# Where the two parts of each weight tile lie against the activations, modulo 256 bytes

## The chip, the cores and the metric

The kernel runs on one core of a Trainium2 chip. The metric is the device time of one execution in microseconds; the time before is the median of three runs.

## The reference, cut to what matters

The reference is a decoder trunk of two layers over 256 tokens of width 2048, in float32. Layer 0 mixes tokens by gated linear attention (GLA), layer 1 by forgetting attention (FoX); each mixer is followed by a gated MLP with a short convolution. Nearly all the arithmetic is in products of the 256 tokens with large weight matrices:

```python
for i in range(DEPTH):                                   # 2 layers
    mod = (cond @ w_mod[i] + b_mod[i])                   # shifts, scales and gates, 6 x 2048, from one vector
    h = rmsnorm(x, norm_mix[i]) * (1.0 + sc_m) + sh_m
    y = gla_mixer(h, ...)  or  fox_mixer(h, ...)         # h @ w_in (2048 x 6160, or 2048 x 8208), attention, @ w_out
    x = x + (1.0 + g_m) * y
    h = rmsnorm(x, norm_ffn[i]) * (1.0 + sc_f) + sh_f
    x = x + (1.0 + g_f) * conv_ffn(h, ...)               # h @ w_up (2048 x 11264), conv, silu(gate) * val, @ w_down (5632 x 2048)
return rmsnorm(x, norm_final)
```

## The kernel before

**The products.** Weights stream from HBM once, in tiles of 128 rows by 1024 columns (512 KB), through a ring of five tiles named `w` that they share with the tiles `wm` of the modulation matrix. `plan` is a list of these tiles in the order of their use, and `next_w` loads them ahead by that list. Each tile is split by `split_w` into two parts of the type float32r: ScalarE casts it to `wh` (L110), VectorE subtracts to get the rest, `wl` (L111). Activations are split in the same manner into a high and a low part (the tiles `h`, made by `make_h`, and `op`, made by `raw_operand`). A product is then three matmuls: high by high, high weight by low activation, low weight by high activation.

**Which operand is held.** A matmul has one operand that is loaded into the array (128 columns, by an instruction LDWEIGHTS of its own, which the profile calls PEld) and one that moves through it. In `stream_a` the weights are held, in blocks of 128 columns, and the 256 tokens move: three matmuls of 256 columns for each block of weights and row tile (L540, L541, L542). It serves nearly everything: the GLA projections but v, both output projections, both MLPs, and the output gate of FoX. In `stream_b` the activations are held and the weights move, 512 columns at a time (L573 to L575): v of GLA and q, k, v of FoX. `narrow` (L587 to L589) serves the projections of 16 columns; it holds weights like `stream_a`.

```python
nc.tensor.matmul(o, wh[:, ms], rh, ...)      # L540, stream_a: out, held, moving; ms = 128 columns, 512 bytes
nc.tensor.matmul(o, wh[:, ms], rl, ...)      # L541
nc.tensor.matmul(o, wl[:, ms], rh, ...)      # L542

cs = slice((k - kts[0]) * nn, (k - kts[0]) * nn + P)   # narrow: nn = 16 columns, a step of 64 bytes for each k
nc.tensor.matmul(pa[:, :T], nh[:, cs], lh, ...)        # L587; L588 has nh and ll, L589 nl and lh
```

**Positions.** Every tile has a fixed byte position in each of the 128 partitions of the on-chip memory. In the program before, the tiles `w`, `h`, `op`, `wh` and `wl` all start at 160 modulo 256 bytes, and the blocks that `stream_a` and `stream_b` take from them step by 512 or 1024 bytes, so a held block and a moving block are always at the same position modulo 256. `narrow` alone is different: its held block lies 64 bytes further for each row tile k, so its offset against the activations runs through 0, 64, 128, 192 and round again. The tiles follow a DMA scratch of 16,384 bytes and fill nearly all that the program may use.

**The order around it.** The program is written out straight, and the order on each engine is set when it is built. `tick` puts a paced share of other work behind each row tile: sums of the modulation vectors on VectorE (L248), convolutions, attention. The buffers hold four tiles each of `wh` and `wl` (AHEAD + 1), so the split runs up to three row tiles ahead of the matmuls; a cast (L110) waits until the matmuls have finished with the buffer that it writes.

Of the kernel before, what the change touches and what calls it, by code (L numbers as in the profile page):

```python
# [59 lines left out]
ORDERED = ("v",)  # L60
NBIG = 12


@with_exitstack
def kernel(
# [37 lines left out]
    def t1(s="t1"):  # L103
        return tmp.tile([P, T], F32, tag="t1", bufs=T1, name=nm(s))

    def split_w(src):
        n_ = src.shape[-1]
        hi = tmp.tile([P, 1024], F32R, tag="wh", bufs=AHEAD + 1, name=nm("wh"))[:, :n_]
        lo = tmp.tile([P, 1024], F32R, tag="wl", bufs=AHEAD + 1, name=nm("wl"))[:, :n_]
        nc.scalar.copy(out=hi, in_=src)  # L110
        order["v"] = nc.vector.tensor_tensor(out=lo, in0=src, in1=hi.bitcast(F32), op=ALU.subtract).ins  # L111
        return hi, lo
# [1 line left out]
    def misc():  # L114
        return psM.tile([P, 512], F32, tag="m" if PS[1] else "a", name=nm("pm"))

# [1 line left out]
    ident = const.tile([P, P], F32, name="ident")  # L118
    make_identity(nc, ident)
    identr = const.tile([FH, FH], F32R, name="identr")  # L120
# [8 lines left out]
    nc.vector.tensor_scalar_mul(mgla, tri, 1.0 / 16.0)  # L129
    nc.vector.memset(mgla[0:CH, CH:P], 0.0)  # L130

# [1 line left out]
    crow = ringt([P, P], "crow")  # L133
    nc.sync.dma_start(out=crow[:KT, :], in_=c.rearrange("b (r p) -> (b r) p", p=P))
    rows = ringt([P, P], "rows")
# [59 lines left out]

    bfc = const.tile([FH, 1], F32, name="bfc")

# [1 line left out]
    mod = const.tile([P, 12, KT], F32, name="mod")  # L199
    bg = deque()  # L200

# [9 lines left out]
        return es  # L211

    def mod_tasks(l, key, f0=0, fn=D, wide=False, direct=0, defer=False):
        # columns of silu(c) @ w_mod + b_mod, finished as the layer uses them;
        # the first `direct` row tiles are summed on the tensor engine, the others on the vector engine
        s = SECT[key]
        width = fn // -(-fn // 1024)
        per = 1
# [120 lines left out]
        pace["bg"] = (len(bg) + len(pending)) / float(n_halves)  # L339
        pace["acc"] = 0.0  # L340

# [1 line left out]
    def rsqrt(dst, src, scale, nn):  # L343
        v = tmp.tile([P, 16], F32, tag="rs_v", name=nm("rv"))
        t = tmp.tile([P, 16], F32, tag="rs_t", name=nm("rt"))
# [19 lines left out]
            nc.tensor.matmul(pb[:, i * P:(i + 1) * P], ones, dg, start=True, stop=True)  # L365
        return pb

# [1 line left out]
    xT = const.tile([P, KT, T], F32, name="xT")  # L369

    def load_x():
# [37 lines left out]
                                              skip_group_check=True).ins  # L409

    def token_rstd():
        # columns of -1/sqrt(mean + eps), one per token tile
        v = tmp.tile([P, 2], F32, tag="tv", name=nm("tv"))
        t = tmp.tile([P, 2], F32, tag="tt", name=nm("tt"))
        q = tmp.tile([P, 2], F32, tag="tq", name=nm("tq"))
        nc.vector.tensor_scalar(out=v, in0=ss["p"][:, :2], scalar1=0.5 / D, scalar2=0.5 * EPS,
                                op0=ALU.mult, op1=ALU.add)
        nc.vector.tensor_scalar(out=q.bitcast(I32), in0=v.bitcast(I32), scalar1=1, scalar2=None,
                                op0=ALU.logical_shift_right)
        nc.vector.tensor_scalar(out=q.bitcast(I32), in0=q.bitcast(I32), scalar1=-1.0,  # L420
                                scalar2=float(0x5F3759DF - 0x00400000), op0=ALU.mult, op1=ALU.add)
        for _ in range(3):
            for i in range(2):
                c1 = slice(i, i + 1)
                nc.vector.tensor_scalar(out=t[:, c1], in0=q[:, c1], scalar1=q[:, c1], scalar2=v[:, c1],
                                        op0=ALU.mult, op1=ALU.mult)
            for i in range(2):
                c1 = slice(i, i + 1)
                nc.vector.tensor_scalar(out=q[:, c1], in0=t[:, c1], scalar1=1.5, scalar2=q[:, c1],
                                        op0=ALU.subtract, op1=ALU.mult)  # L430
        return q
# [48 lines left out]
            return st["t"][:, 0, k % 4, :], st["t"][:, 1, k % 4, :]  # L480
        return lazy(make, nk, 2)

# [1 line left out]
    plan = []  # L484

    def plan_stream(w, kts, cols):
        for kt in kts:
            plan.append((w, kt, 1, tuple(cols)))

    gate = {"n": 0, "ins": []}  # L490
    fetched = {"load": 0, "split": 0, "use": 0}
# [2 lines left out]
    def next_w(kt, cols, hold=None):  # L494
        i = fetched["use"]
        assert plan[i][1] == kt and plan[i][3] == tuple(cols), (plan[i][1:], kt, cols)
        fetched["use"] += 1
        run, look = AHEAD if hold is None else hold, RING - 1
        if i < STAGE:
            run, look = min(run, STAGE - i), 1  # L500
        while fetched["split"] < min(i + 1 + run, len(plan)):
            while fetched["load"] < min(fetched["split"] + look, len(plan)):
                w_, kt_, nk_, cols_ = plan[fetched["load"]]
                fetched["load"] += 1
                wt = ringt([P, 1024])
                o = 0
                for c0, cn in cols_:
                    if nk_ == 1:
                        with after_startup():
                            nc.sync.dma_start(out=wt[:, o:o + cn], in_=w_[kt_ * P:(kt_ + 1) * P, c0:c0 + cn])  # L510
                        o += cn
                    else:
                        nc.sync.dma_start(out=wt[:, :nk_ * cn].rearrange("p (k r) -> p k r", r=cn),
                                          in_=w_[kt_ * P:(kt_ + nk_) * P, c0:c0 + cn]
                                          .rearrange("(k p) r -> p k r", p=P))
                        nc.vector.memset(wt[:, nk_ * cn:nk_ * cn + P - cn], 0.0)
                        o = nk_ * cn + P - cn
                raws.append(wt[:, :o])
            with ExitStack() as es:
                if gate["n"] > 0:  # L520
                    gate["n"] -= 1
                    for ins in gate["ins"]:
                        es.enter_context(tc.issue_after(ins))
                splits.append(split_w(raws.popleft()))
            fetched["split"] += 1
        return splits.popleft()

# [1 line left out]
        return [psA.tile([P, 2, T], F32, tag="a", name=nm("pa")) for _ in range(4)]  # L529

    def stream_a(kts, cols, rhs, done=None):
        # with done: the last TAIL rows are multiplied output by output, so that done(pair) can follow early
        ps = banks()
        held = []

        def mms(m, k, wh, wl, rh, rl):
            first, last = k == kts[0], k == kts[-1]
            ms = slice(m * P, (m + 1) * P)
            o = ps[m // 2][:, m % 2, :]
            nc.tensor.matmul(o, wh[:, ms], rh, start=(first and m % 2 == 0), stop=False, skip_group_check=True)  # L540
            nc.tensor.matmul(o, wh[:, ms], rl, start=False, stop=False, skip_group_check=True)  # L541
            nc.tensor.matmul(o, wl[:, ms], rh, start=False, stop=last, skip_group_check=True)  # L542

        for k in kts:
            rh, rl = rhs(k)
            tail = done is not None and k in kts[-TAIL:]
            wh, wl = next_w(k, cols, kts[-1] - k + 1 if tail else None)
            if tail:
                held.append((k, wh, wl, rh, rl))
                continue  # L550
            for m in range(8):
                mms(m, k, wh, wl, rh, rl)
            tick()
        if done is not None:
            for m in range(8):
                for args in held:
                    mms(m, *args)
                if m % 2 == 1:
                    done(m // 2, ps)
        return ps  # L560
# [50 lines left out]
    ALL = list(range(KT))  # L611

    def log_sigmoid(dst, z, e, bias=None):
        # z may be in PSUM; min(z, 0) - log(1 + exp(-|z|))
        nc.scalar.activation(e, z, AF.Abs)
        nc.scalar.activation(e, e, AF.Exp, scale=-1.0)
        nc.scalar.activation(e, e, AF.Ln, bias=1.0)
        nc.vector.scalar_tensor_tensor(out=dst, in0=z, scalar=0.0, in1=e, op0=ALU.min, op1=ALU.subtract)

# [1 line left out]
    def gla(l, h):  # L621
        parts = {}
        pieces = [("a", 6144), ("q", 0), ("k", 1024), ("v0", 2048), ("v1", 3072), ("r0", 4096), ("r1", 5120)]
# [233 lines left out]
        set_pace(N1)  # L857
        add_residual(l, "g_m", ALL, rhs)

# [1 line left out]
    def fox(l, h):  # L861
        pf = narrow(ALL, 4 * D, FH, h)
        lf = t1("lf")[:FH, :]
# [166 lines left out]
        pace["side"], pace["sacc"] = 1.0, 0.0  # L1030
        add_residual(l, "g_m", ALL, rhs)

# [1 line left out]
    def ffn(l, h, first_blocks):  # L1034
        act = [bigt([P, 8, T], "act") for _ in range((FT + 7) // 8)]

# [76 lines left out]
            cs = slice(m * P, (m + n_) * P)  # L1113
            nc.vector.tensor_tensor(out=fin["o"][tt][:, cs], in0=pt[:, :n_ * P], in1=fin["g"][:, cs], op=ALU.mult)

# [1 line left out]
    def plan_ffn(l):  # L1117
        w = ffn_w_up[l]
        groups = []
# [17 lines left out]
    for nb in BLOCKS:  # L1137
        for i, c0 in enumerate((0, 1024, 2048, 3072, 4096, 5120)):
            if i == (0 if k0 + nb == KT else 1):
                plan.append((gla_w_in[0], k0, nb, ((6144, RANK),)))  # L1140
            plan_stream(gla_w_in[0], range(k0, k0 + nb), [(c0, 1024)])
        k0 += nb
    for g in range(2):
        plan_stream(gla_w_out[0], ALL, [(g * 1024, 1024)])
    plan_ffn(0)
    plan.append((fox_w_in[0], 0, KT, ((4 * D, FH),)))
    for c0 in (2 * D, 2 * D + 1024, 0, D, 1024, D + 1024, 3 * D, 3 * D + 1024):
        plan_stream(fox_w_in[0], ALL, [(c0, 1024)])
    for g in range(2):
        plan_stream(fox_w_out[0], ALL, [(g * 1024, 1024)])  # L1150
    plan_ffn(1)
# [107 lines left out]
```

## Time and profile before

| what | before |
|---|---|
| time, median of 3 runs (range) | 2566.05 us (2564.85 to 2567.67) |
| span of the profiled execution, first to last instruction | 2570.5 us |
| matmuls busy, of the span | 2515.7 us, 98% (19242 matmuls) |
| VectorE busy | 1912.2 us, 74% |
| ScalarE busy | 1280.2 us, 50% |
| HBM traffic | 638 MB, 248 GB/s on average |
| matmuls with held weights in `stream_a` | 3 x (3584 + 1920) = 16512, of 256 columns |
| matmuls with moving weights in `stream_b` | 3 x 512 = 1536, of 512 columns |

The profiled execution has no other time than its span; it is 4.5 us above the median of the timed runs, and above the slowest of them by 2.8 us. Matmuls overlap in the records (each lasts longer than the distance to the next), so what one of them costs is read as the distance between starts in the timeline, not as its duration.

### The profile page before, as it was taken

The page shows a single profiled execution, that of the slowest core. Times are in us where ns is not written, and L with a number is a line of the kernel's source. Part 1 is how long each engine was busy: PE and PEld are TensorE (multiplying, and loading weights), DVE is VectorE, ACT ScalarE, POOL GpSimd, SP SyncE. Part 2 cuts the span into 40 slices and gives each one's busy share as a digit, 9 for nine tenths or more (in the row PEclk, how much of TensorE's full clock was granted, in tenths as well). Part 3 has the DMA queues.
Part 4 walks back from the last instruction along what each step waited for, and adds up shares of the span by engine and source line. Part 5 has one row for each costly group of instructions (what it writes and reads, how often), then busy time and mean ns, then how long its engine had stood idle before and what let it go on. Part 6 is the DMA issues. An engine that isn't in the chain of part 4 may idle for free.

```text
span 2570.5 us, 47584 instructions
## 1 busy us (share of the span) xinstructions
PE 2515.7 (98%) x19242; PEld 2431.0 (95%) x19242; DVE 1912.2 (74%) x2570; ACT 1280.2 (50%) x1956; POOL 14.6 (1%) x35
## 2 busy tenths in 40 slices
PE   6999999999999999999999999999999999999998
PEld 6988899899999999999988889999999999999998
DVE  7767988876679998877587888777766667666544
ACT  2446454445555656543454555444545555565332
POOL 0000000000000000000000000000000000000000
PEclk7999999999999999999999999999999999999999
DMA  8897978798668888889489887686777767756553
GB/s 337 282 301 226 304 245 285 261 321 299 182 183 272 296 295 286 277 310 309 153 285 311 299 265 238 227 278 202 220 223 215 222 212 229 221 183 204 181 181 115
DMA packets 184313, 638.36 MB, mean 248 GB/s; under 512 B 23961, under 2 KB 24971, under 8 KB 183708
## 3 DMA queue, kind: packets, MB, share of 16 engines
q1 hardware_dynamic: 183704, 635.17, 74.9%
q8 instruction: 150, 2.46, 0.4%
q14 instruction: 71, 0.58, 0.1%
q10 hardware_dynamic: 388, 0.15, 0.0%
HBM read 633.14 MB, written 2.10 MB: 247 GB/s over the span
## 4 chain that ended last, share of the span: by engine, by line
PE 85%; DMA 7%; DVE 4%; issue 2%; ACT 1%; DVEq 0%; SPq 0%; ACTq 0%
PE pa L542 23%; PE pa L541 23%; PE pa L540 23%; DMA wm<-in_w_mod_dram 5%; PE pa L574 4%; PE pa L573 4%; PE pa L575 4%; DVE wl L111 2%; DVE acc L248 1%; DMA w<-in_ffn_w_down_dram 1%; DMA w<-in_gla_w_out_dram 1%; ACT wh L110 1%; PE pm L261 1%; DMA w<-in_gla_w_in_dram 0%; PE pm L777 0%
## 5 line engine op out<-in xcount | busy, mean ns | idle before, releaser
L110 ACT CAST wh<-w 128x1024 fp32r<-128x1024 f32 x819 | 855.1, 1047 | 1138.2 <-PE pa L541 677.6
L111 DVE TENSOR_TENSOR wl<-w,wh 128x1024 fp32r<-128x1024 f32 x819 | 995.6, 1219 | 455.7 <-ACT wh L110 444.6
L540 PE MATMUL pa<-h,wh 128*128 128x256 f32 x3584 | 1012.6, 285 | 5.6 <-ACT h L461 5.6
L542 PE MATMUL pa<-h,wl 128*128 128x256 f32 x3584 | 1015.0, 285 | 2.6 <-DVE wl L111 2.6
L541 PE MATMUL pa<-h,wh 128*128 128x256 f32 x3584 | 1015.8, 284 | 1.0 <-DVE h L463 0.9
L540 PEld LDWEIGHTS pa<-h,wh 128*128 128x128 f32 x3584 | 688.0, 193 | 6.8 <-ACT h L461 6.5
L542 PEld LDWEIGHTS pa<-h,wl 128*128 128x128 f32 x3584 | 688.8, 193 | 5.8 <-DVE wl L111 3.3
L541 PEld LDWEIGHTS pa<-h,wh 128*128 128x128 f32 x3584 | 690.1, 193 | 1.7 <-DVE h L463 1.4
L541 PE MATMUL pa<-op,wh 128*128 128x256 f32 x1920 | 540.4, 284 | 1.9 <-DVE op L479 1.9
L540 PE MATMUL pa<-op,wh 128*128 128x256 f32 x1920 | 539.6, 284 | 1.9 <-ACT wh L110 1.6
L248 DVE SCALAR_TENSOR_TENSOR acc<-wm,cT,acc 128x1024 f32<-128x1024 f32 x352 | 450.8, 1281 | 110.0 <-DMA wm<-in_w_mod_dram 109.4
L542 PE MATMUL pa<-op,wl 128*128 128x256 f32 x1920 | 530.2, 284 | 0.1
L541 PEld LDWEIGHTS pa<-op,wh 128*128 128x128 f32 x1920 | 369.3, 192 | 2.1 <-DVE op L479 2.1
L540 PEld LDWEIGHTS pa<-op,wh 128*128 128x128 f32 x1920 | 368.5, 192 | 2.5 <-ACT wh L110 2.0
L542 PEld LDWEIGHTS pa<-op,wl 128*128 128x128 f32 x1920 | 363.1, 192 | 0.7 <-DVE wl L111 0.7
L574 PE MATMUL pa<-wh,h 128*128 128x512 f32 x512 | 201.1, 393 | 0.0
L573 PE MATMUL pa<-wh,h 128*128 128x512 f32 x512 | 199.5, 393 | 0.9 <-ACT wh L110 0.9
L575 PE MATMUL pa<-wl,h 128*128 128x512 f32 x512 | 193.1, 394 | 0.0
L573 PEld LDWEIGHTS pa<-wh,h 128*128 128x128 f32 x512 | 96.6, 189 | 20.8 <-ACT wh L110 1.3
L574 PEld LDWEIGHTS pa<-wh,h 128*128 128x128 f32 x512 | 96.5, 189 | 19.8 <-issue 0.2
L575 PEld LDWEIGHTS pa<-wl,h 128*128 128x128 f32 x512 | 96.2, 189 | 19.1
L1039 ACT ACTIVATE y<-u,cw 128x256 f32<-128x256 f32 x176 | 101.6, 599 | 4.8 <-DVE act L1055 2.4
(236 smaller groups left out, 1389.9 us busy)
## 6 DMA issues: line engine op xcount, KB each, us to landing
wm<-in_w_mod_dram SPq DMA_DIRECT2D x352, 512.0 KB, 5.0
w<-in_ffn_w_up_dram SPq DMA_DIRECT2D x320, 512.0 KB, 4.3
w<-in_ffn_w_down_dram SPq DMA_DIRECT2D x176, 512.0 KB, 4.5
w<-in_fox_w_in_dram SPq DMA_DIRECT2D x128, 512.0 KB, 5.0
w<-in_gla_w_in_dram SPq DMA_DIRECT2D x96, 512.0 KB, 5.1
wm<-in_w_mod_dram SPq DMA_DIRECT2D x16, 1024.0 KB, 12.3
w<-in_gla_w_out_dram SPq DMA_DIRECT2D x32, 512.0 KB, 5.6
w<-in_ffn_w_up_dram SPq DMA_DIRECT2D x64, 256.0 KB, 3.9
```

Of the source, the lines that this page charges most:

```text
L110: nc.scalar.copy(out=hi, in_=src)
L111: order["v"] = nc.vector.tensor_tensor(out=lo, in0=src, in1=hi.bitcast(F32), op=ALU.subtract).ins
L248: nc.vector.scalar_tensor_tensor(out=st["a"], in0=wt[:, j, :], scalar=col, in1=st["a"], op0=ALU.mult, op1=ALU.add)
L261: nc.tensor.transpose(pt[:, m * P:(m + 1) * P], st["a"][:, (q0 + m) * P:(q0 + m + 1) * P], ident)
L540: nc.tensor.matmul(o, wh[:, ms], rh, start=(first and m % 2 == 0), stop=False, skip_group_check=True)
L541: nc.tensor.matmul(o, wh[:, ms], rl, start=False, stop=False, skip_group_check=True)
L542: nc.tensor.matmul(o, wl[:, ms], rh, start=False, stop=last, skip_group_check=True)
L573: nc.tensor.matmul(o, lh[:, ts_], wh[:, hs_], start=first, stop=False)
L574: nc.tensor.matmul(o, ll[:, ts_], wh[:, hs_], start=False, stop=False)
L575: nc.tensor.matmul(o, lh[:, ts_], wl[:, hs_], start=False, stop=last)
L1039: nc.scalar.activation(y, u, AF.Identity, scale=cw[:, l * 3 + 2, r:r + 1], bias=cw[:, 6 + l, r:r + 1])
```

## The change

Each of `wh` and `wl` gets a tile of 1088 columns instead of 1024. Where the weights are held (`moving` is false), the high part is written and read from column 16 on, 64 bytes into its tile, and the low part from column 48 on, 192 bytes into its tile. Where they move, both start at column 0 as before. The plan carries the flag for each tile: true for v of GLA (`c0` 2048 and 3072) and for q, k, v of FoX (`c0` below 3 D). The DMA scratch is reduced from 16,384 to 8,192 bytes; all tiles lie 8,192 bytes lower, which is a multiple of 256, and `h`, `op` and `w` stay at 160 modulo 256.

So for `stream_a` the held `wh` now lies at 224 and the held `wl` at 96 modulo 256, the moving activations at 160 as before. In `stream_b` everything stays at 160. In `narrow` the offsets still step by 64 bytes, from another start.

The instructions of the two programs and their order on each of the five engines are the same; no instruction is added, removed or moved. The diff (comment lines, which the change also removes, are left out):

```diff
+HELD = (16, 48)
+WCOLS = 1024 + 64
...
-    def split_w(src):
+    def split_w(src, moving):
         n_ = src.shape[-1]
-        hi = tmp.tile([P, 1024], F32R, tag="wh", bufs=AHEAD + 1, name=nm("wh"))[:, :n_]
-        lo = tmp.tile([P, 1024], F32R, tag="wl", bufs=AHEAD + 1, name=nm("wl"))[:, :n_]
+        o1, o2 = (0, 0) if moving else HELD
+        hi = tmp.tile([P, WCOLS], F32R, tag="wh", bufs=AHEAD + 1, name=nm("wh"))[:, o1:o1 + n_]
+        lo = tmp.tile([P, WCOLS], F32R, tag="wl", bufs=AHEAD + 1, name=nm("wl"))[:, o2:o2 + n_]
         nc.scalar.copy(out=hi, in_=src)
...
-    def plan_stream(w, kts, cols):
+    def plan_stream(w, kts, cols, moving=False):
         for kt in kts:
-            plan.append((w, kt, 1, tuple(cols)))
+            plan.append((w, kt, 1, tuple(cols), moving))
...
-                w_, kt_, nk_, cols_ = plan[fetched["load"]]
+                w_, kt_, nk_, cols_, mov_ = plan[fetched["load"]]
...
-                raws.append(wt[:, :o])
+                raws.append((wt[:, :o], mov_))
...
-                splits.append(split_w(raws.popleft()))
+                splits.append(split_w(*raws.popleft()))
...
-                plan.append((gla_w_in[0], k0, nb, ((6144, RANK),)))
-            plan_stream(gla_w_in[0], range(k0, k0 + nb), [(c0, 1024)])
+                plan.append((gla_w_in[0], k0, nb, ((6144, RANK),), False))
+            plan_stream(gla_w_in[0], range(k0, k0 + nb), [(c0, 1024)], c0 in (2048, 3072))
...
-    plan.append((fox_w_in[0], 0, KT, ((4 * D, FH),)))
+    plan.append((fox_w_in[0], 0, KT, ((4 * D, FH),), False))
     for c0 in (2 * D, 2 * D + 1024, 0, D, 1024, D + 1024, 3 * D, 3 * D + 1024):
-        plan_stream(fox_w_in[0], ALL, [(c0, 1024)])
+        plan_stream(fox_w_in[0], ALL, [(c0, 1024)], c0 < 3 * D)
...
-    nc = _bacc.Bacc("TRN2", target_bir_lowering=False, num_devices=1)
+    nc = _bacc.Bacc("TRN2", target_bir_lowering=False, num_devices=1, dynamic_dma_scratch_size=8192)
```

## The prediction

> **What bounds the kernel now.** I read the page first: its engine totals, the chain that ended last, then the groups.
>
> ```profile
> span 2570.5 us, 47584 instructions
> PE 2515.7 (98%) x19242; PEld 2431.0 (95%) x19242; DVE 1912.2 (74%) x2570; ACT 1280.2 (50%) x1956; POOL 14.6 (1%) x35
> PE 85%; DMA 7%; DVE 4%; issue 2%; ACT 1%; DVEq 0%; SPq 0%; ACTq 0%
> PE pa L542 23%; PE pa L541 23%; PE pa L540 23%; DMA wm<-in_w_mod_dram 5%; PE pa L574 4%; PE pa L573 4%; PE pa L575 4%; DVE wl L111 2%; DVE acc L248 1%; DMA w<-in_ffn_w_down_dram 1%; DMA w<-in_gla_w_out_dram 1%; ACT wh L110 1%; PE pm L261 1%; DMA w<-in_gla_w_in_dram 0%; PE pm L777 0%
> L110 ACT CAST wh<-w 128x1024 fp32r<-128x1024 f32 x819 | 855.1, 1047 | 1138.2 <-PE pa L541 677.6
> L111 DVE TENSOR_TENSOR wl<-w,wh 128x1024 fp32r<-128x1024 f32 x819 | 995.6, 1219 | 455.7 <-ACT wh L110 444.6
> L540 PE MATMUL pa<-h,wh 128*128 128x256 f32 x3584 | 1012.6, 285 | 5.6 <-ACT h L461 5.6
> ```
>
> The reader should see that the three lines with held weights, L540 to L542, make 69% of the chain, and that most of the cast's idle time is ended by a matmul giving a buffer back: the split waits for TensorE, not the reverse. So the price of a matmul with held weights is the price of the kernel. The group's 285 ns is not that price, since matmuls overlap; the price is the distance between starts, read in the timeline of PE and PEld (columns: start us, duration us, engine, line):
>
> ```profile
> 699.89 0.28 PE L542 MATMUL pa<-h,wl 128*128 128x256 f32 x1
> ...
> 701.09 0.28 PE L540 MATMUL pa<-h,wh 128*128 128x256 f32 x1
> 999.81 0.28 PE L540 MATMUL pa<-h,wh 128*128 128x256 f32 x1
> 999.81 0.19 PEld L541 LDWEIGHTS pa<-h,wh 128*128 128x128 f32 x1
> 1399.90 0.39 PE L573 MATMUL pa<-wh,h 128*128 128x512 f32 x1
> ...
> 1403.98 0.39 PE L573 MATMUL pa<-wh,h 128*128 128x512 f32 x1
> ```
>
> Ten matmuls of 256 columns from 699.89 to 701.09 take 1.20 us: 120.0 ns each. Eighteen of 512 columns from 1399.90 to 1403.98 take 4.08 us: 226.7 ns. The second 256 columns cost 106.7 ns, so a 256-column matmul has 13.3 ns beside its streaming. The rows at 999.81 show that the load of the next weights starts with the running matmul: both read the on-chip memory together, today always at equal positions modulo 256.
>
> Is the supply far enough behind? A row tile (24 matmuls) lasts 24 x 0.120 = 2.88 us.
>
> ```profile
> 100.00:215.00 115.00, 108.76 (x714) 100.26 (x713) 73.84 (x69) 52.10 (x89) 0.00 (x0) 0.97 0.86 285
> 650.00:1055.00 405.00, 405.00 (x3380) 405.00 (x3379) 344.32 (x460) 233.24 (x355) 0.00 (x0) 1.00 0.78 255
> 1055.00:1145.00 90.00, 89.66 (x748) 89.46 (x747) 68.95 (x71) 39.38 (x57) 0.00 (x0) 1.00 0.88 302
> 1800.00:2556.00 756.00, 756.00 (x6306) 756.00 (x6306) 481.00 (x594) 376.69 (x506) 0.00 (x0) 1.00 0.63 201
> ```
>
> These are stages (columns: stretch, its length, busy us of PE, PEld, DVE, ACT, POOL, then clock, DMA share, GB/s). From 650 on PE has no gap and the granted clock is 1.00. VectorE is busy 85% in the fullest stage and 64% in the last one. Before 215 us the kernel goes by its loads: PE is idle there for 6 us of 115, and the chain of waits has pieces such as these:
>
> ```profile
> 138.32 6.29 DMA wm<-in_w_mod_dram
> 180.52 5.39 DMA wm<-in_w_mod_dram
> 1106.08 6.02 DMA wm<-in_w_mod_dram
> ```
>
> **The change, part by part.** *Held weights, the main term.* No matmul, load, split or DMA is added or removed; what can change is the 13.3 ns. The profile of before holds the experiment already, in `narrow`: its held block moves by 64 bytes for each k against the same kind of activations. A load runs beside the matmul before its own, so the three loads of one k lie between the start of the last L589 (or what stands there) and that of its own L589. The rows that bound them:
>
> ```profile
> 88.44 0.28 PE L542 MATMUL pa<-h,wl 128*128 128x256 f32 x1
> 88.56 0.28 PE L587 MATMUL pm<-h,wh 128*128 128x256 f32 x1
> 88.80 0.28 PE L589 MATMUL pm<-h,wl 128*128 128x256 f32 x1
> 89.15 0.28 PE L589 MATMUL pm<-h,wl 128*128 128x256 f32 x1
> 89.51 0.28 PE L589 MATMUL pm<-h,wl 128*128 128x256 f32 x1
> 89.86 0.28 PE L589 MATMUL pm<-h,wl 128*128 128x256 f32 x1
> 90.22 0.28 PE L589 MATMUL pm<-h,wl 128*128 128x256 f32 x1
> 90.57 0.28 PE L589 MATMUL pm<-h,wl 128*128 128x256 f32 x1
> 90.94 0.28 PE L589 MATMUL pm<-h,wl 128*128 128x256 f32 x1
> 91.29 0.28 PE L589 MATMUL pm<-h,wl 128*128 128x256 f32 x1
> ```
>
> Offset by offset, in us for three matmuls: at 0, 0.36 and (89.86 to 90.22) 0.36; at 64, 0.35 and 0.35; at 128, 0.36 and 0.37; at 192, 0.35 and 0.35. The stamps are rounded to 0.01, so the sum is safer: 24 matmuls from 88.44 to 91.29 take 2.85 us instead of 24 x 0.120 = 2.88, 30 ns less. Put down to the four triples at 64 and 192, that is 7.5 ns a triple, 2.5 ns a matmul; at face value these four lose 40 ns and the 128s give 10 back, 3.3 ns a matmul. The changed kernel has `wh` at 64 and `wl` at 192, the two good offsets, in the ratio two to one. I take 7.5 ns a triple, the value that the longer sum carries.
>
> On the chain stand 0.69 x 2570.5 = 1774 us of these lines, 1774 / 0.120 = 14,780 matmuls or 4,927 triples (of 5,504 in all; the other tenth stands where loads set the pace, mostly before 215 us and around 450 and 1100, and gains nothing). 4,927 x 7.5 ns = 37 us.
>
> Bounds of this term: none of the 13.3 ns goes (0), or all of it (14,780 x 13.3 ns = 197 us); below nothing, a triple as at the 128 rows, 10 ns more, 49 us lost.
>
> *Moving weights* (L573 to L575): positions equal as before, so 0. Were they to change, the bounds are 1536 x 13.3 ns = 20 us either way; nothing in the diff moves them.
>
> *Narrow*: 32 triples whose offsets are only permuted: under 0.3 us.
>
> *The split's operands.* The cast writes, and the subtraction reads and writes, at shifted positions. The same 819 instructions at 1047 and 1219 ns; I take 0. What hides them is the matmul stream: in 650 to 1055 VectorE would have to grow by the idle 60.7 us over the stage's 140 row tiles, 0.43 us on each 1.22, before it set the pace. Where the chain does pass through L111 (2%, 51 us), each per cent on its duration is 0.5 us.
>
> *DMA scratch halved, all tiles 8,192 bytes lower.* The loads are issued by SyncE and a few by ScalarE, none by GpSimd, and none of them is in the diff:
>
> ```profile
> w<-in_ffn_w_up_dram SPq DMA_DIRECT2D x320, 512.0 KB, 4.3
> brow<-in_b_mod_dram ACTq DMA_DIRECT2D x2, 48.0 KB, 6.5
> ```
>
> I take 0. If landings did get 10% slower or faster, the chain's 7% of DMA (180 us) would give 18 us either way; the later stages, where DMA is busy 63 to 78%, would hide it.
>
> *What is late next.* A faster stream asks for a row tile every 2.82 us. The stage 1055 to 1145 already moves 302 GB/s and would need 308; the page's first slice shows 337 reached. I allow up to 5 us of the gain to be lost there and near 215, and put none into the sum.
>
> Sum: 2570.5 - 37 = 2533.5 for the span; the median stands 4.5 lower, so 2566 - 37 = **2529 us**.
>
> **The rivals.** *No effect.* The two reads might not touch each other at all, with the narrow rows an accident of other waits; then 2566. [...] Against it: the time for three goes up and down with the offset, twice through the cycle with the same order, with the matmuls otherwise alike. For it: each difference is as small as the stamps' rounding. 0.18.
>
> *A larger gain.* In `narrow` each offset lasts three matmuls only; in a long run the reads may fall into a better step, and half to all of the 13.3 ns could go: 98 to 197 us, 2369 to 2468. The fullest stage allows it (VectorE needs 344.32 / 405 x 2.88 = 2.45 us a row tile, against 24 x 0.1067 = 2.56). For it: the 512-column matmul has the same 13.3 ns though its load is over in half its time, so this looks like a cost of the load's reads. Against it: nothing in the narrow rows comes below 0.35. [...] 0.20.
>
> *Slower: the alternation.* In `narrow` high and low parts have one offset. Here the load of `wl` (beside L541) lies 128 bytes further than the load before, and the next `wh` (beside L542) 128 bytes back. If the distance between successive loads counts as the offset 128 does against the activations, two of three loads are of the bad kind: 90.57 to 90.94 is 0.37, 10 ns over. It decides from the point where a triple takes more than 360 ns; at 5 to 10 ns, 4,927 triples lose 25 to 49 us: 2591 to 2615. 0.12.
>
> **How the numbers follow.** Likeliest, 0.50: a triple is 6 to 10 ns shorter (30 to 49 us), less up to 5 us lost to the supply: 2517 to 2541, with 2529 from the sum. The range has to leave out no more than 0.2: I drop the slower case (0.12) and the far half of the larger gain, and go from 2465 to 2572; the upper end is no effect plus a third of the 18 us on landings. By 0.2% (5 us, about what a measurement of this kernel can tell from no change): faster 0.50 + 0.20 and 0.01 of the no-effect case, 0.71; slower 0.12 + 0.02 of it, 0.14; same 0.15.
>
> **What would show it.** In a stage of held weights, ten starts take 1.17 to 1.18 us instead of 1.20, in L540 to L542 alike; 512-column starts stay at 226.7 ns; L110 and L111 keep 1047 and 1219 ns; PE stays without gaps from 1800 to the end, and that stage shortens by 2%, while the part before 215 us keeps its length. I am wrong if ten starts still take 1.20, if L541 and L542 (beside which `wl`, and `wh` after it, are loaded) cost more than before, or if the starts do shorten and new waits for `wh`, `wl` or loads take the gain back.

## The result, and the profile after

The changed kernel takes 2486.26 us (median of 4 runs, 2485.62 to 2488.58) against 2565.57 us beside it (2564.85 to 2567.67): the ratio is 0.9691, with a 95% interval of 0.9677 to 0.9704. That is 79 us faster, inside the range given, but more than twice the 37 us forecast. The profiled executions stand at 2484.9 and 2570.5 us, 85.6 apart; that of before is a long one for its kernel (the run at 0 below, which has the same step, spans 2563.0 us, 78.1 more than the changed kernel), so what is gained in all is read from the medians.

The page of the changed kernel (lines lie four further down in the file: L544 to L546 are the held products, L577 to L579 the moving ones, L114 and L115 the split):

```profile
PE 2421.4 (97%) x19242; PEld 2331.1 (94%) x19242; DVE 1906.7 (77%) x2570; ACT 1279.8 (52%) x1956; POOL 14.6 (1%) x35
PE 74%; DMA 11%; DVE 9%; issue 3%; ACT 2%; SPq 0%; DVEq 0%; ACTq 0%
PE pa L545 19%; PE pa L546 19%; PE pa L544 19%; DMA wm<-in_w_mod_dram 6%; PE pa L579 4%; PE pa L578 4%; PE pa L577 4%; DVE wl L115 4%; DVE acc L252 2%; DMA w<-in_ffn_w_down_dram 2%; DMA w<-in_ffn_w_up_dram 2%; ACT wh L114 1%; DMA w<-in_gla_w_out_dram 1%; PE pm L265 1%; PE pm L411 0%
L114 ACT CAST wh<-w 128x1024 fp32r<-128x1024 f32 x819 | 856.4, 1048 | 1033.7 <-PE pa L545 463.7
L115 DVE TENSOR_TENSOR wl<-w,wh 128x1024 fp32r<-128x1024 f32 x819 | 994.8, 1218 | 365.0 <-ACT wh L114 354.2
```

The instructions and their counts are those of before, and the split costs what it did (1048 and 1218 ns). The held products have fallen from 69% of the chain to 57%, and loads and VectorE have grown from 11% to 20% (in the profile of the run at 0 they stand at 72% and 6%): part of the kernel is now paced by its supply. The timeline of PE (start us, duration us) shows the new step; first held weights, then moving ones:

```profile
2000.06 0.28 PE L544 MATMUL pa<-h,wh 128*128 128x256 f32 x1
...
2001.20 0.28 PE L545 MATMUL pa<-h,wh 128*128 128x256 f32 x1
1340.16 0.39 PE L577 MATMUL pa<-wh,h 128*128 128x512 f32 x1
...
1345.61 0.39 PE L577 MATMUL pa<-wh,h 128*128 128x512 f32 x1
```

Ten steps of held weights take 1.14 us, and over a long stretch (below) the step is 113.3 ns: 6.7 less than 120.0, just half of the 13.3 ns beside the streaming. Moving weights: 24 steps in 5.45 us, 227 ns as before. Where did 16,512 x 6.67 = 110 us go? The stages that answer to those shown of before, cut at the same matmuls (columns: stretch, length, busy us of PE, PEld, DVE, ACT, POOL, then the granted clock, DMA share, GB/s); the first fence is after, the second before:

```profile
482.20:641.20 159.00, 150.41 (x1275) 149.05 (x1275) 120.58 (x156) 80.12 (x127) 0.00 (x0) 0.96 0.83 281
641.20:1024.50 383.30, 383.11 (x3379) 382.88 (x3378) 339.90 (x456) 231.50 (x354) 0.00 (x0) 1.00 0.82 269
1024.50:1116.70 92.20, 88.00 (x749) 86.82 (x749) 73.16 (x76) 41.42 (x58) 0.00 (x0) 0.98 0.88 303
1756.00:2470.40 714.40, 714.40 (x6306) 714.40 (x6305) 478.75 (x594) 377.25 (x506) 0.00 (x0) 1.00 0.67 213
```

```profile
490.00:650.10 160.10, 156.09 (x1276) 155.50 (x1276) 120.79 (x156) 81.20 (x127) 0.00 (x0) 0.97 0.82 279
650.10:1055.00 404.90, 404.90 (x3379) 404.90 (x3378) 344.22 (x460) 233.24 (x355) 0.00 (x0) 1.00 0.78 255
1800.10:2556.10 756.00, 756.00 (x6307) 756.00 (x6306) 480.90 (x594) 376.69 (x506) 0.00 (x0) 1.00 0.63 201
```

In the two stages without gaps the whole worth arrives: 21.6 us of 3379 x 6.67 = 22.5, and 41.6 of 42.1. The stage after the attention of layer 0 gets 1.1 us of 8.5, with 8.6 us of gaps on PE instead of 4.0. The end of the first MLP, at 302 GB/s before, even gets longer: 90.0 to 92.2 us, with 4.2 us of gaps instead of 0.3. So the step did more than forecast, and the supply took back more.

### The profile page after: what moved, and what is told of

It is laid out like the page before. It is cut to its first block, busy times and chain, and to the rows that moved or that the text cites. A ratio compares the mean times of both kernels' runs of the same rounds, so it can differ in the third digit from the quotient of the medians.

```text
span 2484.9 us, 47584 instructions
## 1 busy us (share of the span) xinstructions
PE 2421.4 (97%) x19242; PEld 2331.1 (94%) x19242; DVE 1906.7 (77%) x2570; ACT 1279.8 (52%) x1956; POOL 14.6 (1%) x35
## 4 chain that ended last, share of the span: by engine, by line
PE 74%; DMA 11%; DVE 9%; issue 3%; ACT 2%; SPq 0%; DVEq 0%; ACTq 0%
PE pa L545 19%; PE pa L546 19%; PE pa L544 19%; DMA wm<-in_w_mod_dram 6%; PE pa L579 4%; PE pa L578 4%; PE pa L577 4%; DVE wl L115 4%; DVE acc L252 2%; DMA w<-in_ffn_w_down_dram 2%; DMA w<-in_ffn_w_up_dram 2%; ACT wh L114 1%; DMA w<-in_gla_w_out_dram 1%; PE pm L265 1%; PE pm L411 0%
## 5 line engine op out<-in xcount | busy, mean ns | idle before, releaser
L114 ACT CAST wh<-w 128x1024 fp32r<-128x1024 f32 x819 | 856.4, 1048 | 1033.7 <-PE pa L545 463.7
L115 DVE TENSOR_TENSOR wl<-w,wh 128x1024 fp32r<-128x1024 f32 x819 | 994.8, 1218 | 365.0 <-ACT wh L114 354.2
L544 PE MATMUL pa<-h,wh 128*128 128x256 f32 x3584 | 990.1, 278 | 10.1 <-ACT h L465 5.6
L545 PE MATMUL pa<-h,wh 128*128 128x256 f32 x3584 | 993.1, 278 | 1.1 <-DVE h L467 0.9
L546 PE MATMUL pa<-h,wl 128*128 128x256 f32 x3584 | 991.7, 278 | 1.5 <-DVE wl L115 1.5
L544 PEld LDWEIGHTS pa<-h,wh 128*128 128x128 f32 x3584 | 674.2, 189 | 12.0 <-ACT h L465 6.6
L546 PEld LDWEIGHTS pa<-h,wl 128*128 128x128 f32 x3584 | 675.0, 189 | 4.4 <-issue 2.3
L545 PEld LDWEIGHTS pa<-h,wh 128*128 128x128 f32 x3584 | 676.9, 189 | 2.0 <-DVE h L467 1.7
L544 PE MATMUL pa<-op,wh 128*128 128x256 f32 x1920 | 527.2, 277 | 5.2 <-DVE xT L600 2.9
L545 PE MATMUL pa<-op,wh 128*128 128x256 f32 x1920 | 526.8, 277 | 2.0 <-DVE op L483 2.0
L546 PE MATMUL pa<-op,wl 128*128 128x256 f32 x1920 | 518.4, 278 | 1.6 <-DVE wl L115 1.0
L544 PEld LDWEIGHTS pa<-op,wh 128*128 128x128 f32 x1920 | 360.8, 188 | 6.6 <-DVE xT L600 3.4
L545 PEld LDWEIGHTS pa<-op,wh 128*128 128x128 f32 x1920 | 361.3, 188 | 2.2 <-DVE op L483 2.2
L546 PEld LDWEIGHTS pa<-op,wl 128*128 128x128 f32 x1920 | 354.9, 188 | 4.3 <-DVE wl L115 4.0
L577 PE MATMUL pa<-wh,h 128*128 128x512 f32 x512 | 199.2, 392 | 0.6 <-ACT wh L114 0.6
L579 PE MATMUL pa<-wl,h 128*128 128x512 f32 x512 | 193.9, 395 | 0.6 <-DVE wl L115 0.5
L577 PEld LDWEIGHTS pa<-wh,h 128*128 128x128 f32 x512 | 96.4, 188 | 20.7 <-ACT wh L114 1.0
L579 PEld LDWEIGHTS pa<-wl,h 128*128 128x128 f32 x512 | 95.9, 188 | 20.8 <-DVE wl L115 2.0
```

What stands on the lines that cost most here:

```text
L577: nc.tensor.matmul(o, lh[:, ts_], wh[:, hs_], start=first, stop=False)
L579: nc.tensor.matmul(o, lh[:, ts_], wl[:, hs_], start=False, stop=last)
```

## The experiments

Every kernel below is the changed one with the edit shown. The step is read in one window of 160 us inside the last MLP, where PE has no gap: 160 us over the count in brackets less the two matmuls on the edges. For the kernel before, and then for the changed one:

```profile
1800.00:1960.00 160.00, 160.00 (x1335) 1.00 0.71 220
```

```profile
1800.00:1960.00 160.00, 160.00 (x1414) 1.00 0.75 235
```

that is 120.0 and 113.3 ns (the columns behind the count: clock, DMA share, GB/s).

**The layout alone, and one place for both parts.**

```diff
-HELD = (16, 48)
+HELD = (0, 0)        # e1_zero; (16, 16) in e2_both64, (48, 48) in e3_both192, (32, 32) in e4_both128
```

> Both parts of the weights at 0 (HELD = (0, 0)), with the longer tiles and the halved scratch kept: the layout alone. All theories that hold the position against the activations responsible: 120.0 ns from start to start in stages of held weights, the kernel at 2566 us. If the lower addresses or the scratch carry the gain: 113.3 ns and 2486 us.

> Both parts at 64 bytes. Theory 1 (the price depends only on where the loaded block lies against the moving one, and 64 is a good place): 113.3 ns, 2486 us. Theory 2 (the gain needs two successive loads 128 bytes apart, as wh and wl are in the changed kernel; at a constant 64 the price is that of the narrow rows of before, 117.5 ns): 117.5 ns, about 2535 us.

> Both parts at 192 bytes. Theory 1: 113.3 ns, 2486 us. Theory 2: 117.5 ns, about 2535 us.

> Both parts at 128 bytes. Theory 1, read with the narrow rows of before (0.36 and 0.37 us for three): 120 ns, 2566 us. Theory 3 (any place but the same one will do): 113.3 ns, 2486 us. Theory 2: 120 ns.

Measured: at 0, 2564.60 us (ratio to the kernel before 0.9993, 0.9982 to 1.0005); both at 64, 2503.08 (0.9747, 0.9686 to 0.9808); both at 192, 2532.99 (0.9863, 0.9828 to 0.9899); both at 128, 2550.09 (0.9933, 0.9908 to 0.9957). The windows, in this order; of both at 64 two stretches:

```profile
1800.00:1960.00 160.00, 160.00 (x1336) 1.00 0.72 224
```

```profile
1800.00:1960.00 160.00, 160.00 (x1414) 1.00 0.75 233
2000.00:2160.00 160.00, 160.00 (x1361) 1.00 0.71 222
```

```profile
1800.00:1960.00 160.00, 160.00 (x1361) 1.00 0.72 226
```

```profile
1800.00:1960.00 160.00, 160.00 (x1351) 1.00 0.72 223
```

At 0 the step is 119.9 ns: the lower addresses, the longer tiles and the halved scratch do nothing. At 192 it is 117.7, near the 117.5 that the narrow rows of before had given; at 128 it is 118.6, less than the 120 expected from those rows. At 64 it is 113.3 ns in one stretch and 117.7 in the next, with the same instructions at the same places. The rows between the two show what lies there (the last row of the first stretch, eight transposes, the first of the second):

```profile
1972.74 0.28 PE L544 MATMUL pa<-h,wh 128*128 128x256 f32 x1
1972.85 1.03 PE L265 MATMUL pm<-ident,acc 128*128 128x128 f32 x8
1973.64 0.36 PE L545 MATMUL pa<-h,wh 128*128 128x256 f32 x1
```

So a stream with both parts at 64 has two steps, keeps the one that it has over hundreds of matmuls, and can leave an interruption with the other. The run with both at 192 has the short step too, though only near its end:

```profile
2430.00:2510.00 80.00, 80.00 (x708) 80.00 (x707) 35.45 (x29) 29.37 (x28) 0.00 (x0) 1.00 0.50 163
```

That is 113.3 ns, where the window at 1800 shows 117.7. Neither theory had this. Theory 1 (the place alone sets the price) falls, since one place has two prices; theory 3 (any other place will do) falls with 128, whose trace has no stretch at 113.3.

**Other pairs of places.**

```diff
-HELD = (16, 48)
+HELD = (48, 16)      # e7_swap; (0, 32) in e10_0_128, (0, 48) in e6_lo192
```

> The two places exchanged: high part at 192, low part at 64. Theory 2 (two successive loads 128 bytes apart, neither at the place of the moving operand, keep the stream in its short step): 113.3 ns everywhere, about 2486 us. Theory 5 (each part has its own good place): more than 113.3 ns, between 117.5 and 120, 2530 us or more.

> High part at 0, low part at 128: again 128 bytes between the two loads, but both at the places that were bad when constant (120.0 and 118.8 ns). Theory 2a (the distance of 128 between successive loads is what counts): 113.3 ns, 2486 us. Theory 2b (the places 64 and 192 count as well): 118 to 120 ns, 2545 to 2566 us.

> Only the low part moved, to 192; the high part at 0. Theory 1 (each load has its price by its own place): two of three matmuls carry a load at 0 for 120.0 ns, one a load at 192 for 113 to 117.5, mean 117.8 to 119.2, about 2540 to 2555 us. Theory 2: loads 64 bytes apart, no settled short step, 117 to 120 ns. If the alternation of any two places is enough: 113.3 ns, 2486 us.

One run each: 2496.05, 2552.75 and 2536.11 us, beside 2566.08 for the kernel before. The windows, of the exchanged pair two stretches:

```profile
1800.00:1960.00 160.00, 160.00 (x1414) 1.00 0.75 234
2000.00:2160.00 160.00, 160.00 (x1348) 1.00 0.71 222
```

```profile
1800.00:1960.00 160.00, 160.00 (x1346) 1.00 0.71 222
```

```profile
1800.00:1960.00 160.00, 160.00 (x1361) 1.00 0.73 226
```

The exchanged pair has 113.3 ns in one stretch and 118.9 in the next; 0 with 128 has 119.0, so 128 bytes between the parts are not enough (theory 2a falls); 0 with 192 has 117.7, close to theory 1 and theory 2 alike. Neither expectation for the exchanged pair came, since it has both steps. Of the pairs tried, 64 for the high part and 192 for the low part is the one that holds the short step (6306 matmuls in the 714.4 us of the stage shown above are 113.3 ns each).

The exchanged pair and the changed kernel can also come back to the short step with no interruption. In the exchanged pair, ten steps take 1.20 us before 654.62 and 1.13 from 655.08 on, with nothing but the same three matmuls between (first fence, rows left out at the dots); in the changed kernel, a longer step at 1693.37 is followed by slow ones, nine steps in 1.08 us, and then by seven in 0.79 (second fence):

```profile
653.42 0.28 PE L546 MATMUL pa<-h,wl 128*128 128x256 f32 x1
...
654.62 0.40 PE L544 MATMUL pa<-h,wh 128*128 128x256 f32 x2
...
655.08 0.28 PE L544 MATMUL pa<-h,wh 128*128 128x256 f32 x1
...
656.21 0.28 PE L546 MATMUL pa<-h,wl 128*128 128x256 f32 x1
```

```profile
1693.37 0.29 PE L544 MATMUL pa<-op,wh 128*128 128x256 f32 x1
...
1694.45 0.28 PE L544 MATMUL pa<-op,wh 128*128 128x256 f32 x1
...
1695.24 0.28 PE L545 MATMUL pa<-op,wh 128*128 128x256 f32 x1
```

**What the place is counted in.**

```diff
-HELD = (16, 48)
-WCOLS = 1024 + 64
+HELD = (80, 112)     # m1_plus256; in m2_32_160 (8, 40), WCOLS as it was
+WCOLS = 1024 + 128
```

> The changed kernel with 256 bytes more on both offsets: high part at 320, low part at 448. If only the position modulo 256 counts: steps of 113.3 ns, 2486 us. If the offset itself or a longer period counts: another step, 117.5 to 120 ns, 2530 to 2566 us.

> High part at 32, low part at 160 bytes: the same 128 bytes between the parts, half way between the places tried. If places are told apart in units of 64 bytes: this reads as 0 and 128 do, 119 ns, about 2553 us. If it is the bytes themselves and a distance of 128 off the bad place is what counts: near 113.3 ns, 2486 us; between the two, 116 ns.

With 256 bytes more the kernel takes 2487.57 us (one run) at 113.3 ns, as the changed one: these two places repeat after 256 bytes. At 32 and 160 it takes 2542.70 us (one run). The windows, in this order:

```profile
1800.00:1960.00 160.00, 160.00 (x1414) 1.00 0.75 234
```

```profile
1800.00:1960.00 160.00, 160.00 (x1354) 1.00 0.72 224
```

The second is 118.3 ns, near what 0 and 128 have and far from the short step. That agrees with places told apart by 64 bytes, though one pair doesn't prove the unit.

**The moving weights shifted as well.**

```diff
-        o1, o2 = (0, 0) if moving else HELD
+        o1, o2 = HELD
```

> The weights that move (v of GLA; q, k, v of FoX) shifted as the held ones are; the held ones as in the changed kernel. If the place of the moving operand against the held activations counts there as elsewhere: 512-column matmuls leave 226.7 ns, for 220 (10 us faster, 2476) or upward (up to 10 us slower, 2496). If the 13.3 ns of a 512-column matmul have another cause: 226.7 ns and 2486 us.

2493.84 us in one run (span 2492.1 against 2484.9). The 512-column steps grow; 24 of them, from the first row to the second, take 5.53 us, 230.4 ns instead of 227.1:

```profile
1340.41 0.39 PE L578 MATMUL pa<-wh,h 128*128 128x512 f32 x1
...
1345.94 0.39 PE L578 MATMUL pa<-wh,h 128*128 128x512 f32 x1
```

1536 x 3.3 ns = 5 us of the 7 in the spans. Where the weights move, equal places are better than 64 and 192; so the flag in the plan is worth something, and what a place is worth differs between the two kinds of matmul.

**Where the rest of the 110 us went.** All modulation tiles behind the start-up are read from one tile that is loaded once, so these kernels leave out most of the modulation matrix and serve for timing alone:

```diff
+    fix = {}
...
+                if not wide:
...
+                    if "t" not in fix:
+                        fix["t"] = const.tile([P, 1, 1024], F32, name="wmfix")
+                        nc.sync.dma_start(out=fix["t"][:, 0, :], in_=w_mod[0, 0:P, 0:1024])
+                    st[kt] = fix["t"]
+                    return
```

> The changed kernel without the loads of the modulation tiles behind the start-up: all their sums read one tile that is loaded once, so VectorE does the same work and some 180 MB less is moved. Compare with its pair at 0 (next). If the loads' rate is what gave back the part of the 110 us that didn't arrive, the pair differs by 103 to 110 us; if VectorE's work did it, by 86 us as the changed kernel and the one before do.

> The same without those loads, both parts of the weights at 0: the pair to the one before. Loads' rate: 103 to 110 us slower than it; VectorE's work: 86 us slower. Steps of 120.0 ns in held stages by either.

2449.60 us with the places of the change (ratio 0.9547, 0.9519 to 0.9574) and 2555.81 with both at 0 (0.9956, 0.9940 to 0.9972): 106.2 us apart, against 79 with the loads. VectorE's busy time is the same 1906.7 us as in the changed kernel. The stages of the first (the stretches after the attention and at the end of the first MLP) have hardly a gap any more:

```profile
474.00:632.00 158.00, 157.78 (x1391) 157.58 (x1390) 122.89 (x137) 84.48 (x130) 0.00 (x0) 1.00 0.65 195
1006.00:1090.00 84.00, 84.00 (x743) 84.00 (x743) 69.94 (x70) 38.47 (x55) 0.00 (x0) 1.00 0.60 199
```

So the loads took back the missing part, not VectorE's sums. The two pairs also tell where. The first 3200 matmuls, in the run at 0, in the changed kernel, and without the loads at 0 and at the places of the change (columns: stretch, length, busy us of PE, clock, DMA share, GB/s):

```profile
0.00:468.50 468.50, 443.28 (x3200) 0.96 0.85 291
0.00:468.60 468.60, 437.06 (x3200) 0.95 0.85 291
0.00:462.50 462.50, 440.67 (x3201) 0.96 0.60 194
0.00:449.20 449.20, 426.96 (x3200) 0.96 0.62 199
```

With the loads, the new step gains nothing in the first 468 us; without them it gains 13. Removing the loads is worth 9 us at the old step (2564.60 to 2555.81, across two sets of runs) and 37 at the new one: the same loads cost four times as much once the matmuls are shorter.

**A better supply.** Single late loads or their rate?

```diff
-RING = 5
+RING = 6             # s1_ring6 and s3_ring6_slow
-SLOW = 0.0
+SLOW = 0.3           # s2_slow, s3_ring6_slow, b2_slow30; 0.45 in b1_slow45
-AHEAD = 3
+AHEAD = 4            # s4_ahead4, with dynamic_dma_scratch_size=2048
```

> The changed kernel with a ring of six weight tiles instead of five (loads issued one tile further ahead). The shorter matmul step is worth 16,512 x 6.67 = 110 us, of which 85.6 came through; 23.5 us turned into new gaps of TensorE in stages fed by loads. If these gaps come from late single loads, a deeper ring takes half of them or more back: 2470 to 2478 us. If they come from the rate of the loads in those stages: 2484 to 2488 us, no change.

> The changed kernel with the modulation work started 48 row tiles earlier in the MLP of layer 0 (SLOW = 0.3 instead of 0, in a stage that moves 195 to 207 GB/s), which leaves less of it for the stage up to its end (296 to 316 GB/s). If the rate of the loads takes the gain back between 850 and 1117 us, up to 9 us (7.0 lost at 1025 to 1117, 0.8 and some more around it) return: 2477 to 2482 us. If single late loads do it: no change, 2486.

> Both: a ring of six and SLOW = 0.3. The sum of the two effects where they are independent: by the rate theory 2477 to 2482 us, by the theory of single late loads 2470 to 2478 us, with both true below 2470.

> The changed kernel with five buffers each of the split weights instead of four (AHEAD = 4), and the DMA scratch at 2,048 bytes to make room. If the supply fails by single late tiles, a fourth row tile in hand covers 2.7 us more of lateness: 2472 to 2480 us. If by rate: 2484 to 2488. If the scratch size mattered to any transfer, landings (5.0 us for the modulation tiles) would leave their value.

| kernel | median us | ratio to before, 95% interval |
|---|---|---|
| the changed kernel | 2486.26 | 0.9691 (0.9677 to 0.9704) |
| ring of 6 | 2482.92 | 0.9683 (0.9663 to 0.9703) |
| SLOW = 0.3 | 2475.85 | 0.9650 (0.9636 to 0.9665) |
| ring of 6 and SLOW = 0.3 | 2478.17 | 0.9658 (0.9643 to 0.9672) |
| AHEAD = 4, scratch 2,048 | 2492.77 | 0.9713 (0.9699 to 0.9727) |

More depth does not help: the ring of six can't be told from the changed kernel, and five split buffers are no faster (6.5 us slower, though the intervals touch, and the smaller scratch is part of that run). Starting the modulation work earlier helps, 10 us. Its stage at the end of the first MLP, the last row against 92.20 us of the changed kernel and 90.0 of the kernel before:

```profile
480.00:638.90 158.90, 150.97 (x1296) 149.84 (x1297) 122.45 (x160) 82.09 (x134) 0.00 (x0) 0.97 0.83 285
638.90:1021.60 382.70, 382.70 (x3379) 382.70 (x3379) 344.88 (x464) 233.05 (x355) 0.00 (x0) 1.00 0.84 277
1021.60:1106.00 84.40, 84.40 (x747) 84.40 (x747) 66.95 (x70) 39.70 (x57) 0.00 (x0) 1.00 0.90 307
```

The gaps there are gone, at much the same rate of loads (307 GB/s against 303) with less to load; those of the first row stay. One more step in that direction, with its pair on the same chip:

> The changed kernel with the modulation work started earlier still (SLOW = 0.45). At 0.3 the kernel was 10 us faster than the changed kernel, with the stage that had lost time (92.1 us) down to 84.5. If more evenness helps: 2470 to 2475 us; if the stage is no longer the limit at 0.3, or the earlier stage now pays: 2475 to 2480.

> SLOW = 0.3 once more beside it, for the comparison of the two on one chip: 2474 to 2478 us.

0.45 gave 2475.72 us (0.9650, 0.9636 to 0.9665), 0.3 gave 2478.11 (0.9656, 0.9642 to 0.9669): the same. With the run above, these two settings are 87 to 91 us faster than the kernel before beside them, the best versions of this study that do all the work.

## Why the prediction was wrong in size

**The bound.** Right: TensorE's stream of held products set the time, and a change of 6.67 ns in its step came out nearly in full in the two stages where PE has hardly a gap (21.6 of 22.5 us from 641 on, 41.6 of 42.1 from 1756 on).

**The direction and the cause.** Right: the 13.3 ns beside the streaming depend on where the loaded block lies. The run at 0 (2564.60 us, 0.9993 of the kernel before) shows that nothing else in the change matters. The no-effect rival falls: the same matmuls take 120.0 or 113.3 ns by the bytes at which the held blocks start. That it is their place *against the moving operand* that counts is argued, not shown: no run moves the activations, which stay at 160, so the held block's own place would explain the held products as well. What makes the difference inside the chip isn't seen in any trace.

**The size of the main term: here is the failed step.** I took 7.5 ns a triple from four narrow triples, "the two good offsets, in the ratio two to one". It measured 20 ns a triple (360 to 340). The narrow rows were not wrong: the 117.5 ns that their sum gave is near the longer of the two steps that long streams at these places have (117.7). The wrong part was to take the step of three matmuls at an offset for the one step of a long stream there. With both at 64, or both at 192, the stream has a step of 113.3 and one of 117.7; so a constant place does not rule the short step out, and only long stretches show it. What 64 and 192 in turn add is that the stream stays in it (6306 matmuls in 714.4 us).

**The rival "slower: the alternation".** It named the right peculiarity, two places in turn, with the wrong sign. The larger-gain rival, whose lower end was half of the 13.3 ns and 98 us, described the step exactly, and its reason, that a long run may fall into a better step, is what the runs show; it had 0.20. The measured time lies inside the range only because the range took in the near half of this rival, not by the sum. Its argument against, that nothing in the narrow rows comes below 0.35, rested on three matmuls at each offset. One reading for it was wrong: the load of a 512-column matmul is not over in half its time, since it lasts 189 ns of a step of 227. The far half of its range was not reached: the shortest step in the windows is 113.3 ns.

**The supply.** I allowed up to 5 us to be lost. On the chain's 14,780 matmuls the new step is worth 14,780 x 6.67 = 98.6 us; the medians differ by 79, so about 19 were lost, 31 of the 110 that all matmuls together are worth (28 by the pair without the loads, 106.2 against 78.3). The 13 lost before 468 us are near the tenth of the matmuls that the prediction had left out (1732 x 6.67 = 11.6 us). Of the rest, some 7 us each went in two stages: one was not named (490 to 650), and one was (1055 to 1145) but priced too low: at a step of 113.3 the last 90 us of the first MLP would need 302 x 120 / 113.3 = 320 GB/s, and got 303. The 337 GB/s that I took for reserve came from the start-up, where 16 of the modulation loads have 1024 KB instead of 512.

**Terms at nothing.** The split's operands (1048 and 1218 ns), the moving weights (227 ns) and the scratch were rightly put at 0; for moving weights the experiment gives the price that the bound of 20 us left open, 5 to 7 us.

**Open.** Why 64 and 192 in this order hold the short step, and the reverse order, 64 alone or 192 alone only in some stretches, isn't settled. The runs show two lasting steps, changes at interruptions, and returns to the short step without one; they don't show what makes the difference. A run with the activations moved, and the held blocks with them, would tell the distance between the operands from the place itself.

## What to carry to other kernels

When a stream of equal matmuls steps longer than its columns explain (here 120.0 ns, where 256 more columns in one matmul cost 106.7), note the byte positions of the held and the moving operand modulo 256 and try a few offsets: here it cost a few columns of padding, some room from the DMA scratch, and no instruction. Try them in the stream itself and over hundreds of matmuls, because a few rows at one offset can show one of two lasting steps (here the narrow rows gave 117.5 ns, and a stream with both parts at 64 had 113.3 and 117.7). And when the bound gets shorter, price the next limit stage by stage: here an even pace of the background loads was worth 10 us more, and deeper buffers nothing that could be told.

## What the runs showed of the hardware that was not expected

- A stream of identical 256-column matmuls with held blocks at 64 bytes off stepped 113.3 ns for one stretch and 117.7 for the next, with eight transposes between them.
- With held blocks at equal, 64, 128 and 192 bytes off, the step was 119.9, 113.3 or 117.7, 118.6, and 117.7 or (at the end) 113.3 ns; with 64 and 192 in turn 113.3, with 32 and 160 118.3.
- For 512-column matmuls equal places were better (227.1 ns) than 64 and 192 in turn (230.4 ns).
- A DMA scratch of 8,192 bytes instead of 16,384 changed nothing measurable (0.9993, 0.9982 to 1.0005, together with the rest of the layout).
